# Down projection of a decoder block: seven products for eight on six of eleven weight tiles

## The chip, the cores and the metric

One core of one Trainium2 chip runs the whole block. The core has five engines that run side by side, each through its own queue of instructions in order: TensorE (PE in the profile; PEld is its weight load), VectorE (DVE), ScalarE (ACT), GpSimd (POOL) and SyncE (SP), which here only issues DMAs. The matrix products accumulate in PSUM, eight banks of 128 x 512 fp32 numbers; everything else lies in SBUF. The metric is the device time of one execution in microseconds, the median of several runs.

## What is computed

One layer on 256 tokens of width 1024, all in fp32: two token mixers (a gated linear recurrence and a block-sparse attention) side by side, their merge, a first layer norm, a gated feed-forward network (FFN) and a second layer norm. The part that matters here is the last:

```python
x = layer_norm(DN_ALPHA * x + mixed, ln1_w, ln1_b)
h = jnp.einsum('bsd,df->bsf', x, w_ffn_in)
h_gate, h_up = jnp.split(h, 2, axis=-1)
y = jnp.einsum('bsf,fd->bsd', jax.nn.silu(h_gate) * h_up, w_ffn_down)
return layer_norm(DN_ALPHA * x + y, ln2_w, ln2_b)
```

The hidden width is 2816, that is 22 rows of 128 features. The down projection multiplies 256 x 2816 activations by 2816 x 1024 weights.

## The kernel before

**Halves.** TensorE takes its operands in a rounded 32-bit form (float32r). To keep fp32 accuracy, every operand is split: the high half is a cast on ScalarE, the low half is the operand less that cast, a subtraction on VectorE (`split`, lines 168 to 170). One product of two fp32 matrices is then three matmuls: high by high, high by low, low by high (lines 676 to 678).

**Weights.** `plan` lists all weight tiles in the order of use, 1 MB each (128 partitions x 2048 fp32). `stage` (line 176) loads the next one on SP's queue into one of three `raw` buffers, casts it on ScalarE into one of four `h` buffers (line 192) and subtracts on VectorE into one of four `l` buffers (line 194). `fetch` (line 198) hands out the next staged tile and first stages until three more are ready behind it. So the tile three ahead is written into the buffers of the tile before the current one.

**FFN.** For each pair of feature rows j (line 810) one tile of gate weights and one of up weights are fetched; `wide_pair` makes two PSUM tiles of each (two for the gate from the pool `mm`, two for up from `aux`, four banks each). ScalarE copies half of a PSUM tile out, VectorE adds the other half (lines 817, 818), ScalarE applies the SiLU, VectorE multiplies gate by up, and the product is split into `ah` and `al` for the down projection. The first two pairs are done earlier, for each half of the tokens (`FfnEarly`).

**Down projection.** Eleven tiles q of two feature rows by 1024 columns. For each tile, `rows_pass` multiplies both feature rows, for 128 tokens and for two column halves of 512: eight products of 128 x 128 by 128 x 512 in all, 24 matmuls, into four PSUM banks. For the last three tiles (`HOLD_DOWN`) the products of the second half of the tokens are put off to the end, so that the second layer norm of the first half runs beside them. The last 256 columns of that go to a bank of their own, `more`.

**Second layer norm.** For each half of the tokens: residual times alpha plus PSUM (line 685), statistics (688, 690), a power on GpSimd (692), two scalings with the broadcast weights `wb2` (695, 698), two stores. `bcast` loads such weights through GpSimd's queue.

**Order.** A planner orders the instructions of each engine by a timing model. Inside `tc.manual_schedule(engines=...)` the engines named take their instructions in the order in which the program writes them. Before the change that holds for the output projection and the early FFN pairs, and for TensorE alone in the held part at the end.

**SBUF.** A pool `big` of twelve 8 KB buffers (`slot`) holds the larger arrays; a buffer is handed on when its last reader is done.

Of the kernel before, what the change touches and what calls it, by code (L numbers as in the profile page):

```python
# [71 lines left out]
def plan():  # L72

    tiles = []

    def add(w, k0, kn, c0, n, held=False):
        tiles.append((w, k0, kn, c0 if isinstance(c0, tuple) else (c0,), n, held))

    def feat(w, c0, n):
        for c in range(c0, c0 + n, 256):  # L80
            add(w, 0, 8, c, 256)

    def tok(w, c0, n):
        for c in range(c0, c0 + n, 512):
            add(w, 0, 4, c, 512)
            add(w, 4, 4, c, 512)

    feat("w_in", 0, 1024)
    tok("w_in", 2048, 1024)
    tok("w_in", 3072, 1024)  # L90
    tok("w_in", 6144, 512)
    tok("w_in", 8192, 1024)
    for c in range(2):
        if c == 1:
            tok("w_in", 6144 + 512, 512)
        for j in range(2 * c, 2 * c + 2):
            feat("w_in", 5120 + j * 256, 256)
            feat("w_in", 4096 + j * 256, 256)
    tok("w_in", 7168, 1024)
    tok("w_branch_a", 0, 1024)  # L100
    tok("w_branch_b", 0, 1024)
    for k in range(0, KC, 2):
        add("w_out", k, 2, 0, 1024)
    for j in range(0, EARLY, 2):
        for k in range(0, KC, 4):
            add("w_ffn_in", k, 4, (j * P, FF + j * P), 256, j < HOLD_IN)
    for j in range(EARLY, NF, 2):
        add("w_ffn_in", 0, 8, j * P, 256)
        add("w_ffn_in", 0, 8, FF + j * P, 256)
    for k in range(0, NF, 2):  # L110
        add("w_ffn_down", k, 2, 0, 1024)
    return tiles


# [1 line left out]
def hybrid_layer_kernel(ctx: ExitStack, tc, x, xw, vecs, bias, wts, ln1_w, ln1_b, ln2_w, ln2_b, consts, out):  # L116
# [12 lines left out]
    def slot(name, dt=F32):  # L129
        return big.tile([P, 2048], dt, tag="s8", name=name)  # L130

    def r32(ap):
        return ap.bitcast(F32)
# [27 lines left out]
                return self.pair[self.u, ks, ts]  # L161


    loads = plan()
    ready = []
    state = {"next": 0}

    def split(dst_h, dst_l, src):
        nc.scalar.copy(dst_h, src)
        nc.vector.tensor_sub(dst_l, src, r32(dst_h))  # L170
# [5 lines left out]
    def stage(pieces=None, eng=nc.vector):  # L176
        i = state["next"]
        if i >= len(loads):
            return
        state["next"] += 1  # L180
        _, _, k, _, _, held = loads[i]
        src = wts[i].rearrange("p (k c) -> p k c", k=k)
        view = lambda z: z.rearrange("p (k c) -> p k c", k=k)
        raw = view(wraw.tile([P, 2048], F32, tag="raw", name=f"raw{i}"))
        if held:
            h, l = view(slot(f"wh{i}", F32R)), view(slot(f"wl{i}", F32R))
        else:
            h = view(whi.tile([P, 2048], F32R, tag="h", name=f"wh{i}"))
            l = view(wlo.tile([P, 2048], F32R, tag="l", name=f"wl{i}"))
        for ks in ks_of(pieces or (k,)):  # L190
            nc.sync.dma_start(raw[:, ks, :], src[:, ks, :])
            nc.scalar.copy(h[:, ks, :], raw[:, ks, :])  # L192
            yield
            eng.tensor_sub(l[:, ks, :], raw[:, ks, :], r32(h[:, ks, :]))  # L194
# [465 lines left out]
    def bcast(name, w, b):  # L660
        t = slot(name).rearrange("p (a d) -> p a d", a=2)
        nc.gpsimd.dma_start(t[:, 0, :], w[0].partition_broadcast(P))
        nc.gpsimd.dma_start(t[:, 1, :], b[0].partition_broadcast(P))
        return t
# [12 lines left out]
                    nc.tensor.matmul(ps, lh(kk)[:, ts], wl[:, k, ns], start=False, stop=False)  # L677
                    nc.tensor.matmul(ps, ll(kk)[:, ts], wh[:, k, ns], start=False, stop=(kk == ktot - 1))  # L678

    def layer_norm(name, t, parts, res, wb, r, store=None, more=None):  # L680

        stats = sm.tile([P, len(parts), 6], F32, tag="bst", name=f"{name}s{t}")
        for i, (ps, n0) in enumerate(parts):
            ns = slice(n0, n0 + ps.shape[1])
            nc.vector.scalar_tensor_tensor(r[:, ns], res[:, ns], ALPHA, ps, op0=ALU.mult, op1=ALU.add)
            if more is not None and i == len(parts) - 1:
                nc.vector.tensor_add(r[:, ns], r[:, ns], more)
            nc.vector.bn_stats(stats[:, i, :], r[:, ns])
        ag = sm.tile([P, 4], F32, tag="bag", name=f"{name}a{t}")
        nc.vector.bn_aggr(ag[:, 0:2], stats)  # L690
# [24 lines left out]
    ah = [slot(f"ah{i}", F32R).rearrange("p (k t) -> p k t", k=KC) for i in range(3)]  # L715
    al = [slot(f"al{i}", F32R).rearrange("p (k t) -> p k t", k=KC) for i in range(3)]

    def norm1(t):
        layer_norm("n1", t, pss[t], xr[:, t, :], wb1, x1[:, t, :])
# [11 lines left out]
    class FfnEarly:  # L731
# [74 lines left out]
    e[1][1].transpose()  # L806


    room = slot("room").rearrange("p (i f t) -> p i f t", i=4, f=2)
    for j in range(EARLY, NF, 2):  # L810
        n = j // 2 % 2
        sums = []
        for i, (nm, p, tag) in enumerate([("g", mm, "mm"), ("u", aux, "aux")]):
            pss = wide_pair(f"f{nm}{j}", x1p, p, tag)
            s = room[:, 2 * i + n, :, :]
            for f, ps in enumerate(pss):
                nc.scalar.copy(s[:, f, :], ps[:, 1, :])
                nc.vector.tensor_add(s[:, f, :], ps[:, 0, :], s[:, f, :])
            if i == 0:
                nc.scalar.activation(s, s, AF.Silu)  # L820
            sums.append(s)
        nc.vector.tensor_mul(sums[0], sums[0], sums[1])
        i, k = divmod(j, KC)
        split(ah[i][:, k:k + 2, :], al[i][:, k:k + 2, :], sums[0])

    pss = [row_parts("wd0", [(aux, 512)] * 2), row_parts("wd1", [(aux, 512)] * 2)]
    lhs = (lambda kk: ah[kk // KC][:, kk % KC, :], lambda kk: al[kk // KC][:, kk % KC, :])
    y = slot("y").rearrange("p (t d) -> p t d", t=NT)
    tiles = []
    for q in range(NF // 2):  # L830
        tiles.append((2 * q,) + fetch())
        rows_pass(pss[0], lhs, 0, tiles[-1:], NF)
        if q < NF // 2 - HOLD_DOWN:
            rows_pass(pss[1], lhs, 1, tiles[-1:], NF)
    layer_norm("n2", 0, pss[0], x1[:, 0, :], wb2, y[:, 0, :], store=out[0:P, :])

    left, (bank, n0) = pss[1]
    more = mm.tile([P, 256], F32, tag="mm", name="more")
    held = tiles[-HOLD_DOWN:]
    with tc.manual_schedule(engines={ET.PE}):  # L840
        rows_pass([left, (bank[:, 0:256], n0)], lhs, 1, held, NF)
        rows_pass([(more, n0 + 256)], lhs, 1, held, NF, first=held[0][0])
    layer_norm("n2", 1, [left, (bank[:, 0:256], n0), (bank[:, 256:512], n0 + 256)], x1[:, 1, :], wb2, y[:, 1, :],
               store=out[P:T, :], more=more)


_INS = ['x', 'xw', 'vecs', 'bias', 'wts', 'ln1_w', 'ln1_b', 'ln2_w', 'ln2_b', 'consts']
# [32 lines left out]
```

## Time and profile before

| | |
|---|---|
| median of three runs | 500.73 us (500.57 to 501.01) |
| profiled execution, first to last instruction | 498.3 us |
| TensorE busy | 490.4 us, 2728 matmuls |
| VectorE busy | 355.8 us, 424 instructions |
| ScalarE busy | 265.0 us, 328 instructions |
| HBM read | 91.17 MB |
| FFN's last product, start | 430.8 us |
| down projection's last product, start | 490.93 us |

The profile is one execution, times counted from its first instruction. A timeline row has the start, the duration, the engine, the line, the operation, its output and inputs, and in brackets how long the engine stood idle before it and what released it. Matmuls overlap in the pipe, so the distance from start to start says how fast they go, not the printed duration. In a group's row the numbers behind the bar are busy time in all, mean nanoseconds of one, and idle time before with its releasers. The granted clock is the share of TensorE's full clock that it was allowed.

### The profile page before, as it was taken

The numbers are of one execution on the slowest core, as the hardware profiler recorded it, in microseconds if no ns is written. First come the engines' busy times: TensorE is split into PE (matmuls) and PEld (weight loads), VectorE is DVE, ScalarE is ACT, GpSimd is POOL, SyncE is SP. The second block draws the span as 40 slices with busy tenths as digits, with TensorE's granted clock in tenths as the row PEclk, the third lists the DMA queues.
The fourth block names the chain that finished last, engine by engine and source line by source line (L and its number), as shares of the span: only waits on it lengthen the run. The fifth ranks groups of instructions, "written<-read, shape, count | busy, mean of one in ns | idle before, by whom it ended". The sixth has DMA issues, their size and how long they took to land.

```text
span 498.3 us, 6753 instructions
## 1 busy us (share of the span) xinstructions
PE 490.4 (98%) x2728; PEld 427.8 (86%) x2728; DVE 355.8 (71%) x424; ACT 265.0 (53%) x328; POOL 34.0 (7%) x33
## 2 busy tenths in 40 slices
PE   9999999999999999999999999999999999999994
PEld 9999888888899888888888888888888888888884
DVE  4886799999867796886586778854766656644436
ACT  6794487434547676668654353445655565443300
POOL 0000000000004622331000001000000000000000
PEclk9999999999999999999999999999999999999998
DMA  8967436634442436447664454354654555437002
GB/s 306 422 228 308 169 99 245 232 142 170 168 170 86 170 136 245 151 172 279 244 210 176 166 196 181 110 230 167 236 187 169 191 211 190 168 120 292 13 0 84
DMA packets 14558, 92.65 MB, mean 186 GB/s; under 512 B 1728, under 2 KB 1728, under 8 KB 4672
## 3 DMA queue, kind: packets, MB, share of 16 engines
q1 hardware_dynamic: 13680, 89.08, 48.8%
q0 software_dynamic: 848, 3.15, 1.8%
q8 instruction: 21, 0.34, 0.3%
q14 instruction: 9, 0.07, 0.0%
HBM read 91.17 MB, written 1.05 MB: 185 GB/s over the span
## 4 chain that ended last, share of the span: by engine, by line
PE 98%; DVE 1%; DVEq 0%; issue 0%
PE fu L253 7%; PE fg L253 7%; PE wd L678 4%; PE wd L677 4%; PE wd L676 4%; PE fg L254 3%; PE fu L254 3%; PE mq L253 2%; PE mk L253 2%; PE sc L428 2%; PE hq L265 2%; PE hq L264 2%; PE hq L263 2%; PE za L295 1%; PE za L293 1%; PE mv L293 1%
## 5 line engine op out<-in xcount | busy, mean ns | idle before, releaser
L194 DVE TENSOR_TENSOR wl<-raw,wh 128x2048 fp32r<-128x2048 f32 x77 | 178.1, 2318 | 93.1 <-ACT wh L192 93.0
L192 ACT CAST wh<-raw 128x2048 fp32r<-128x2048 f32 x77 | 146.9, 1917 | 93.8 <-PE wd L678 18.7
L253 PE MATMUL fg<-x1p,wh 128*128 128x512 f32 x144 | 50.5, 394 | 0.0
L253 PE MATMUL fu<-x1p,wh 128*128 128x512 f32 x144 | 50.4, 394 | 0.0
L254 PE MATMUL fg<-x1p,wl 128*128 128x256 f32 x144 | 40.0, 278 | 0.0
L254 PE MATMUL fu<-x1p,wl 128*128 128x256 f32 x144 | 39.9, 277 | 0.0
L678 PE MATMUL wd<-wh,al 128*128 128x512 f32 (+1 forms) x88 | 33.6, 382 | 0.0
L677 PE MATMUL wd<-wl,ah 128*128 128x512 f32 (+1 forms) x88 | 33.6, 382 | 0.0
L676 PE MATMUL wd<-wh,ah 128*128 128x512 f32 (+1 forms) x88 | 33.4, 382 | 0.0
L253 PEld LDWEIGHTS fu<-x1p,wh 128*128 128x128 f32 x144 | 27.0, 187 | 6.2
L253 PEld LDWEIGHTS fg<-x1p,wh 128*128 128x128 f32 x144 | 27.0, 187 | 6.1
L254 PEld LDWEIGHTS fg<-x1p,wl 128*128 128x128 f32 x144 | 27.1, 188 | 0.1
L254 PEld LDWEIGHTS fu<-x1p,wl 128*128 128x128 f32 x144 | 27.1, 188 | 0.0
L676 PEld LDWEIGHTS wd<-wh,ah 128*128 128x128 f32 x88 | 16.5, 188 | 3.3
L677 PEld LDWEIGHTS wd<-wl,ah 128*128 128x128 f32 x88 | 16.5, 188 | 3.2
L678 PEld LDWEIGHTS wd<-wh,al 128*128 128x128 f32 x88 | 16.5, 188 | 3.2
L263 PE MATMUL hq<-xp,wh 128*128 128x256 f32 x64 | 18.1, 283 | 0.0
L264 PE MATMUL hq<-xp,wh 128*128 128x256 f32 x64 | 18.1, 283 | 0.0
L265 PE MATMUL hq<-xp,wl 128*128 128x256 f32 x64 | 18.1, 283 | 0.0
L253 PE MATMUL mk<-xp,wh 128*128 128x512 f32 x48 | 17.5, 402 | 0.0
L253 PE MATMUL mq<-xp,wh 128*128 128x512 f32 x48 | 17.2, 399 | 0.0
L430 DVE COPY_PREDICATED SD<-cst,sc 128x512 f32<-128x512 uint32 x14 | 14.9, 1068 | 1.3 <-PE sc L428 1.0
(269 smaller groups left out, 1192.5 us busy)
## 6 DMA issues: line engine op xcount, KB each, us to landing
raw<-in_wts_dram SPq DMA_DIRECT2D x77, 1024.0 KB, 4.8
xw<-in_xw_dram SPq DMA_DIRECT2D x6, 640.0 KB, 9.3
xr<-in_x_dram POOLq DMA_DIRECT2D x1, 1024.0 KB, 5.5
wb<-in_ln_w_dram POOLq DMA_DIRECT2D x2, 512.0 KB, 5.3
wb<-in_ln_b_dram POOLq DMA_DIRECT2D x2, 512.0 KB, 7.2
out_dram<-y SPq DMA_DIRECT2D x4, 256.0 KB, 2.0
cst<-in_consts_dram SPq DMA_DIRECT2D x1, 960.0 KB, 14.7
xw<-in_xw_dram SPq DMA_DIRECT2D x2, 384.0 KB, 4.0
```

The costliest lines, as they stand in the source:

```text
L192: nc.scalar.copy(h[:, ks, :], raw[:, ks, :])
L194: eng.tensor_sub(l[:, ks, :], raw[:, ks, :], r32(h[:, ks, :]))
L253: nc.tensor.matmul(ps, wh[:, k, wcol], a.both(k), start=(k == 0), stop=False)
L254: nc.tensor.matmul(ps[:, 0, :], wl[:, k, wcol], a[0, k, slice(0, T)], start=False, stop=(k == KC - 1))
L263: nc.tensor.matmul(ps, wh[:, k, wcol], ah[:, kk, :], start=(kk == 0), stop=False)
L264: nc.tensor.matmul(ps, wh[:, k, wcol], al[:, kk, :], start=False, stop=False)
L265: nc.tensor.matmul(ps, wl[:, k, wcol], ah[:, kk, :], start=False, stop=(kk == KC - 1))
L293: nc.tensor.matmul(pss[t], ah[:, kk, ts], wh[:, k, :], start=(kk == 0), stop=False)
L430: nc.vector.copy_predicated(later(SD, n, 4 * g, 4), m[:, None, :, :, :].to_broadcast([P, 4, nb, NT, n]), ps.rearrange("p a (b u i) -> p a ...
L676: nc.tensor.matmul(ps, lh(kk)[:, ts], wh[:, k, ns], start=(kk == first), stop=False)
L677: nc.tensor.matmul(ps, lh(kk)[:, ts], wl[:, k, ns], start=False, stop=False)
L678: nc.tensor.matmul(ps, ll(kk)[:, ts], wh[:, k, ns], start=False, stop=(kk == ktot - 1))
```

## The change

Six tiles of the down projection, q = 2 to 7 (`FAST`), use a scheme of seven products for eight (a Winograd form of Strassen's). A tile's product is read as a 2 x 2 block product: activations in four blocks of 128 x 128 (two halves of the tokens by two feature rows), weights in four corners of 128 x 512 (two feature rows by two column halves).

- **Activations.** In the FFN steps of these tiles VectorE forms four sums and differences of the blocks, each 128 x 128, and the seven blocks are split in halves (896 columns, where 512 were split).
- **Weights.** Each of these tiles is staged twice, from one load. The stage "corners" forms the two differences at once (1024 columns), a further sum and difference (512 each), and splits three corners (1536 columns). The stage "sums" splits the four sums (twice 1024 columns). Both take an `h` and an `l` buffer. The sums lie in constants that are no longer read (`cst`) and in an old buffer (`mv1`).
- **Products.** Three with the corners, four with the sums, three matmuls each. Products 1, 5, 6 and 7 are shared by several outputs and have banks of their own, `p1`, `p5`, `p6`, `p7`; 2, 3 and 4 go straight into the accumulators that plain tiles use too (`p2`, `p3`, `p4`; `wd0` takes plain products alone). All eight banks are in use.
- **Shared products.** After the last of the six tiles `into_residual` adds them into the residual `x1`, which takes its factor alpha there: eight operations of 512 columns on VectorE and a copy on ScalarE. The second layer norm then has alpha 1.
- **Order of tiles.** `DOWN = "SSPSSPSSPPP"`: q = 2, 3, 0, 4, 5, 1, 6, 7, 8, 9, 10. The last three are plain and held as before. The loads follow this order.
- **Written order.** The last two FFN steps and the down projection up to the held part are inside `manual_schedule` for TensorE, VectorE and ScalarE.
- **Moved.** The load of `wb2` goes from before the output projection to behind the FFN; the bank `more` comes from `aux`.

```diff
+ORDERED = 2
+DOWN = "SSPSSPSSPPP"
+FAST = tuple(range(2, 2 + DOWN.count("S")))
...
+    for i, (w, k0, k, _, _, held) in enumerate(plan()):
+        fast = w == "w_ffn_down" and k0 // 2 in FAST
+        loads += [(i, k, held, kind) for kind in (("corners", "sums") if fast else ("plain",))]
...
+    def stage_fast(i, kind):
+        view = lambda z: z.rearrange("p (b c) -> p b c", b=4)
+        h = whi.tile([P, 2048], F32R, tag="h", name=f"wh{kind}{i}")
+        l = wlo.tile([P, 2048], F32R, tag="l", name=f"wl{kind}{i}")
+        if kind == "corners":
+            b = view(wraw.tile([P, 2048], F32, tag="raw", name=f"raw{i}"))
+            nc.sync.dma_start(b, view(wts[i]))
+            y, z = corners[i] = [v.rearrange("p (b c) -> p b c", b=2) for v in (
+                cst[:, C_COS:C_COS + D], cp.tile([P, D], F32, tag="mv1", name=f"sums{i}"))]
+            nc.vector.tensor_sub(y, b[:, 1:3, :], b[:, 0:1, :].to_broadcast([P, 2, 512]))
+            h, l = view(h)[:, 0:3, :], view(l)[:, 0:3, :]
+            nc.scalar.copy(h, b[:, 1:4, :])
+            yield
+            nc.vector.tensor_add(z[:, 0, :], b[:, 2, :], y[:, 0, :])
+            nc.vector.tensor_sub(z[:, 1, :], b[:, 3, :], z[:, 0, :])
+            nc.vector.tensor_sub(l, b[:, 1:4, :], r32(h))
+            yield
+        else:
+            h, l = view(h), view(l)
+            for z, bs in zip(corners.pop(i), (slice(0, 2), slice(2, 4))):
+                nc.scalar.copy(h[:, bs, :], z)
+                yield
+                nc.vector.tensor_sub(l[:, bs, :], z, r32(h[:, bs, :]))
+                yield
+        ready.append((h, l))
...
-    wb2 = bcast("wb2", ln2_w, ln2_b)
...
+        nc.vector.tensor_mul(gate, gate, up)
+        if q in PLAIN:
+            split(act_plain[q][:, 0], act_plain[q][:, 1], gate)
+            return
+        nc.vector.tensor_add(z[:, 4, :], z[:, 0, :], z[:, 2, :])
+        nc.vector.tensor_sub(z[:, 5, :], z[:, 4, :], z[:, 1, :])
+        nc.vector.tensor_sub(z[:, 6, :], z[:, 1, :], z[:, 0, :])
+        nc.vector.tensor_sub(z[:, 7, :], z[:, 3, :], z[:, 5, :])
+        act_fast[q] = fast_parts(FAST.index(q))
+        split(*act_fast[q], z[:, 1:8, :])
...
+    with tc.manual_schedule(engines={ET.PE, ET.DVE, ET.Activation}):
+        for j in range(NF - 2 * ORDERED, NF, 2):
+            ffn_step(j)
+        wb2 = bcast("wb2", ln2_w, ln2_b)
...
+        def fast(q):
+            ah, al = act_fast[q]
+            for products in [((p1, 0, 0), (p2, 2, 2), (p3, 6, 1)),
+                             ((p4, 1, 3), (p5, 3, 0), (p6, 4, 2), (p7, 5, 1))]:
+                wh, wl = fetch()
+                for ps, a, b in products:
+                    stop = q == FAST[-1] and ps in shared
+                    nc.tensor.matmul(ps, ah[:, a, :], wh[:, b, :], start=(q == begins[id(ps)]), stop=False)
+                    nc.tensor.matmul(ps, ah[:, a, :], wl[:, b, :], start=False, stop=False)
+                    nc.tensor.matmul(ps, al[:, a, :], wh[:, b, :], start=False, stop=stop)
+
+        def into_residual():
+            u = slot("u").rearrange("p (b c) -> p b c", b=4)
+            first, second = slice(0, 512), slice(512, D)
+            res = lambda t, ns, z: nc.vector.scalar_tensor_tensor(x1[:, t, ns], x1[:, t, ns], ALPHA, z,
+                                                                  op0=ALU.mult, op1=ALU.add)
+            nc.scalar.copy(u[:, 0, :], p1)
+            res(1, second, p1)
+            nc.vector.tensor_add(u[:, 1, :], p6, u[:, 0, :])
+            nc.vector.tensor_add(u[:, 2, :], p7, u[:, 1, :])
+            nc.vector.tensor_sub(u[:, 3, :], u[:, 1, :], p5)
+            res(1, first, u[:, 3, :])
+            res(0, second, u[:, 2, :])
+            nc.vector.tensor_sub(u[:, 0, :], u[:, 2, :], p5)
+            res(0, first, u[:, 0, :])
...
+        for i, q in enumerate(SEQUENCE):
+            if q in FAST:
+                fast(q)
+                if q == FAST[-1]:
+                    into_residual()
+                continue
+            tile_q = [(2 * q,) + fetch()]
+            if i < len(SEQUENCE) - HOLD_DOWN:
+                for part in late:
+                    rows_pass([part], lhs, 1, tile_q, first=2 * begins[id(part[0])], **ends)
+            else:
+                held += tile_q
+            for part in early:
+                rows_pass([part], lhs, 0, tile_q, first=2 * begins[id(part[0])], **ends)
...
-    more = mm.tile([P, 256], F32, tag="mm", name="more")
+    more = aux.tile([P, 256], F32, tag="aux", name="more")
```

More of the change, by code (lines that the diff above doesn't have):

```diff
@@ L37 @@
 HOLD_DOWN = 3
+ORDERED = 2
+DOWN = "SSPSSPSSPPP"
+FAST = tuple(range(2, 2 + DOWN.count("S")))
+PLAIN = tuple(q for q in range(NF // 2) if q not in FAST)
+SEQUENCE = [(FAST if s == "S" else PLAIN)[DOWN[:i].count(s)] for i, s in enumerate(DOWN)]
 C_ID = 0
@@ L109, in plan @@
         add("w_ffn_in", 0, 8, FF + j * P, 256)
-    for k in range(0, NF, 2):
-        add("w_ffn_down", k, 2, 0, 1024)
+    for q in SEQUENCE:
+        add("w_ffn_down", 2 * q, 2, 0, 1024)
     return tiles
@@ L180, in stage @@
         state["next"] += 1
-        _, _, k, _, _, held = loads[i]
+        i, k, held, kind = loads[i]
+        if kind != "plain":
+            list(stage_fast(i, kind))
+            return
         src = wts[i].rearrange("p (k c) -> p k c", k=k)
@@ L714, in hybrid_layer_kernel, with fast_parts @@
     x1p = Pair("x1p")
-    ah = [slot(f"ah{i}", F32R).rearrange("p (k t) -> p k t", k=KC) for i in range(3)]
-    al = [slot(f"al{i}", F32R).rearrange("p (k t) -> p k t", k=KC) for i in range(3)]
+    apl = [slot(f"ap{i}", F32R).rearrange("p (q u k t) -> p q u k t", q=2, u=2, k=2)
+           for i in range((len(PLAIN) + 1) // 2)]
+    act_plain = {q: apl[i // 2][:, i % 2] for i, q in enumerate(PLAIN)}
+    def fast_parts(i):
+        if i == 0:
+            tiles = [klp.tile([P, H * P], F32R, tag="kl", name="ash"), cp.tile([P, D], F32R, tag="bgr", name="asl")]
+        else:
+            both = slot(f"as{i}", F32R)
+            tiles = [both[:, 0:1024], both[:, 1024:2048]]
+        return [z[:, 0:7 * P].rearrange("p (b t) -> p b t", b=7) for z in tiles]
+    act_fast = {}
     def norm1(t):
@@ L806, in hybrid_layer_kernel, with ffn_step @@
     e[1][1].transpose()
[L809 to L816, printed above, removed]
+    room = slot("room").rearrange("p (n b t) -> p n b t", n=2, b=8)
+    def ffn_step(j):
+        q = j // 2
+        z = room[:, q % 2]
+        gate, up = [z[:, b:b + 4, :].rearrange("p (f t) c -> p f (t c)", f=2) for b in (0, 4)]
+        for nm, p, tag, s in [("g", mm, "mm", gate), ("u", aux, "aux", up)]:
+            for f, ps in enumerate(wide_pair(f"f{nm}{j}", x1p, p, tag)):
@@ L817, in hybrid_layer_kernel @@
                 nc.scalar.copy(s[:, f, :], ps[:, 1, :])
                 nc.vector.tensor_add(s[:, f, :], ps[:, 0, :], s[:, f, :])
-            if i == 0:
+            if nm == "g":
                 nc.scalar.activation(s, s, AF.Silu)
[L821 to L826, printed above, removed]
@@ new lines, in hybrid_layer_kernel @@
+    for j in range(EARLY, NF - 2 * ORDERED, 2):
+        ffn_step(j)
+    with tc.manual_schedule(engines={ET.PE, ET.DVE, ET.Activation}):
+        for j in range(NF - 2 * ORDERED, NF, 2):
+            ffn_step(j)
+        wb2 = bcast("wb2", ln2_w, ln2_b)
+        bank = lambda p, n: p.tile([P, 512], F32, tag="aux" if p is aux else "mm", name=n)
+        p2, p4, p1, p5 = [bank(mm, f"wp{i}") for i in (2, 4, 1, 5)]
+        p7, p3, wd0, p6 = [bank(aux, f"wp{i}") for i in (7, 3, 0, 6)]
+        shared = (p1, p5, p6, p7)
+        lhs = (lambda kk: act_plain[kk // 2][:, 0, kk % 2, :], lambda kk: act_plain[kk // 2][:, 1, kk % 2, :])
+        late, early = [(p2, 512), (p3, 0)], [(p4, 512), (wd0, 0)]
+        ends = dict(ktot=2 * PLAIN[-1] + 2)
+        begins = {id(ps): SEQUENCE[0] for ps in (p2, p3, p4)}
+        begins.update({id(wd0): PLAIN[0]})
+        begins.update({id(ps): FAST[0] for ps in shared})
+        def fast(q):
[22 more added lines that the diff above has]
+            res(0, first, u[:, 0, :])
+        held = []
+        for i, q in enumerate(SEQUENCE):
[8 more added lines that the diff above has]
+                    rows_pass([part], lhs, 1, tile_q, first=2 * begins[id(part[0])], **ends)
+            else:
+                held += tile_q
+            for part in early:
+                rows_pass([part], lhs, 0, tile_q, first=2 * begins[id(part[0])], **ends)
@@ L840, in hybrid_layer_kernel @@
+    y = slot("y").rearrange("p (t d) -> p t d", t=NT)
+    layer_norm("n2", 0, [(wd0, 0), (p4, 512)], x1[:, 0, :], wb2, y[:, 0, :], alpha=1.0, store=out[0:P, :])
+    more = aux.tile([P, 256], F32, tag="aux", name="more")
     with tc.manual_schedule(engines={ET.PE}):
[L841 to L844, printed above, removed]
+        rows_pass([(p3, 0), (p2[:, 0:256], 512)], lhs, 1, held, first=None, **ends)
+        rows_pass([(more, 768)], lhs, 1, held, first=held[0][0], **ends)
@@ L847 @@
+    layer_norm("n2", 1, [(p3, 0), (p2[:, 0:256], 512), (p2[:, 256:512], 768)], x1[:, 1, :], wb2, y[:, 1, :],
+               alpha=1.0, store=out[P:T, :], more=more)
 _INS = ['x', 'xw', 'vecs', 'bias', 'wts', 'ln1_w', 'ln1_b', 'ln2_w', 'ln2_b', 'consts']
```

22 lines of the change are left out of this document (7 added, 15 removed).

## The prediction

> **What bounds the kernel now.** I read the page's first two parts, then the chain that ended last, then the busy times of the last seventy microseconds by stretch, then the timelines of TensorE, VectorE (DVE) and ScalarE (ACT) there.
>
> ```profile
> span 498.3 us, 6753 instructions
> PE 490.4 (98%) x2728; PEld 427.8 (86%) x2728; DVE 355.8 (71%) x424; ACT 265.0 (53%) x328; POOL 34.0 (7%) x33
> PE 98%; DVE 1%; DVEq 0%; issue 0%
> ```
>
> The chain is TensorE from the start nearly to the end. The down projection is the last matrix stage, so its stretches say who has room (columns: length, then busy time of PE, PEld, DVE, ACT, POOL; granted clock; DMA share; GB/s):
>
> ```profile
> 400.00:410.00 10.00, 10.00 (x59) 8.77 (x58) 6.81 (x8) 5.23 (x7) 0.00 (x0) 1.00 0.45 156
> 440.00:450.00 10.00, 10.00 (x45) 8.27 (x45) 5.01 (x3) 5.64 (x3) 0.00 (x0) 1.00 0.29 108
> 460.00:470.00 10.00, 10.00 (x46) 8.29 (x45) 4.59 (x2) 2.95 (x3) 0.00 (x0) 1.00 0.13 54
> 470.00:480.00 10.00, 10.00 (x46) 8.28 (x45) 2.29 (x1) 1.17 (x1) 0.00 (x0) 1.00 0.00 1
> ```
>
> TensorE is full at granted clock 1.00, DVE half idle. The two ends of the stage and its last handover:
>
> ```profile
> 429.91 0.40 PE L253 MATMUL fu<-x1p,wh 128*128 128x512 f32 x1
> ...
> 430.95 0.39 PE L676 MATMUL wd<-wh,ah 128*128 128x512 f32 x1
> ...
> 486.74 0.28 PE L676 MATMUL wd<-wh,ah 128*128 128x256 f32 x1
> ...
> 490.93 0.28 PE L678 MATMUL more<-wh,al 128*128 128x256 f32 x1
> 491.25 0.42 DVE L687 TENSOR_TENSOR y<-y,more 128x256 f32<-128x256 f32 x1 [1.07 <-PE more L678]
> 491.70 0.43 DVE L688 BATCH_NORM_STATS2 n2s<-y 128x6 f32<-128x256 f32 x1
> 492.17 0.24 DVE L690 BATCH_NORM_AGGREGATE n2a<-n2s 128x2 f32<-128x18 f32 x1
> ```
>
> Between 430.95 and 486.74 lie 246 products of 512 columns: 55.79/246 = 0.2268 us each, well under the printed 0.39, which overlaps. The 35 steps from 486.74 to 490.93 make 0.120 us for 256 columns; 429.91 to 430.95 are three pairs of the FFN, 0.347 each. The DVE add of `more` starts 0.2 us after the last product's slot ends (491.05), and from the aggregate at 492.17 to the span's end are 498.3 - 492.17 = 6.13 us, which the change leaves alone. So the end is: that add's start + 0.92 + 6.13.
>
> **The change, part by part.**
>
> *TensorE.* A fast tile issues 3 + 4 products of three matmuls, 21 instead of 24, all of 512 columns. Six tiles save 18 x 0.2268 = **4.08 us**, the ceiling. Weight loads fall in step. The eight accumulators take all eight banks; of the FFN's last banks only those of its last `fu` tile are emptied late (about 432, below), and the products that may need them start after 432.99. I cost that at nothing.
>
> *What DVE and ACT pay.* Durations and queue steps come from these rows of the groups and the timeline:
>
> ```profile
> L194 DVE TENSOR_TENSOR wl<-raw,wh 128x2048 fp32r<-128x2048 f32 x17 | 38.9, 2292 | 39.7 <-ACT wh L192 39.7
> L170 DVE TENSOR_TENSOR fl<-xw,fh 128x1024 fp32r<-128x1024 f32 x6 | 7.4, 1226 | 1.4 <-ACT fh L169 1.3
> L440 DVE TENSOR_TENSOR Tt<-Tt 128x128 f32<-128x128 f32 x1 | 0.3, 291 | 0.0
> L402 DVE TENSOR_TENSOR SD<-sd,cst 128x512 f32<-128x512 f32 x4 | 2.6, 680 | 0.0
> L818 DVE TENSOR_TENSOR room<-fu,room 128x256 f32<-128x256 f32 x11 | 4.6, 417 | 0.0
> L817 ACT COPY room<-fu 128x256 f32<-128x256 f32 x10 | 3.7, 366 | 1.0 <-PE fu L254 1.0
> L169 ACT CAST ah<-room 128x512 fp32r<-128x512 f32 x9 | 5.6, 623 | 3.3 <-DVE room L822 3.2
> L169 ACT CAST fh<-xw 128x1024 fp32r<-128x1024 f32 x6 | 6.3, 1046 | 0.0
> L192 ACT CAST wh<-raw 128x2048 fp32r<-128x2048 f32 x17 | 32.4, 1913 | 33.8 <-PE wd L678 18.7 <-PE fg L253 11.4 <-issue 2.2
> ```
> ```profile
> 443.55 4.49 DVE L194 TENSOR_TENSOR wl<-raw,wh 128x2048 fp32r<-128x2048 f32 x2 [5.84 <-ACT wh L192]
> ...
> 481.50 0.69 DVE L685 SCALAR_TENSOR_TENSOR y<-x,wd 128x512 f32<-128x512 f32 x1 [8.00 <-PE wd L678]
> 482.22 0.69 DVE L688 BATCH_NORM_STATS2 n2s<-y 128x6 f32<-128x512 f32 x1
> 482.86 0.69 DVE L685 SCALAR_TENSOR_TENSOR y<-x,wd 128x512 f32<-128x512 f32 x1
> ...
> 487.27 0.68 DVE L685 SCALAR_TENSOR_TENSOR y<-x,wd 128x512 f32<-128x512 f32 x1
> 487.98 0.69 DVE L688 BATCH_NORM_STATS2 n2s<-y 128x6 f32<-128x512 f32 x1
> ```
>
> Two independent subtractions of 2048 columns take 4.49, so one moves the queue by 4.49 - 2.29 = 2.20, 0.08 under its duration (482.22 to 482.86 shows the same for 512). An operation that needs the one just before it starts 0.03 after that one's end (481.50 + 0.69 to 482.22). No row has 1536 columns: it lies between 1.23 (1024) and 2.29 (2048); as 512 to 1024 adds 0.55 and 1024 to 2048 adds 1.07, twice as much, I take the middle, 1.76. On ACT likewise 1.48. The broadcast operand costs nothing extra in the L402 row.
>
> One fast tile on DVE: differences of corners 1.25 (the next needs it), add 0.71, subtract 0.60, low half of three corners 1.68, two low halves of the sums 2 x 1.14: **6.5 us, where a plain tile has 2.20**. TensorE takes 21 x 0.2268 = 4.76 for that tile and 5.44 for a plain one, so two fast and one plain tile cost DVE 15.2 and TensorE 15.0: **the two engines are level**, and the lead built up before counts. ACT has 1.48 + 2 x 1.05 per fast tile, 9.1 in 15 us, and stays ahead.
>
> *The lead.* Each fetch stages three loads ahead, into the buffers of the load before the current one. In the FFN's last two steps, now in written order, the first corners, sums and second corners are staged, each when a product group of the FFN (16 pairs, 5.55) frees its buffers, and behind the emptying of the group before:
>
> - first corners: group ends 414.3, + 0.2 + copy 0.37 + add 0.45, + 1.25 + 0.71 + 0.60 + 1.76 = 419.6, wanted at 430.95
> - first sums: group ends 419.85, + 0.2 + 0.37 + 0.45 + product 0.71 + cast 0.62 + first sum's cast 0.95 (it steps 0.10 early) + two waits of 0.03 = 423.2, + 1.14 + 1.23 = 425.6, wanted at 433.0
> - second corners: two adds of 0.33 behind that, + 4.32 = 430.6, wanted at 435.7
> - second sums: the same chain as for the first from 430.95 gives 434.3, + 2.37 = 436.7, wanted at 437.75
>
> DVE has no pause of note after that, but for the casts named. Finish against need:
>
> - plain 439.4 (0.5 of it waiting for its cast, which stands behind the sums' two) / 440.5
> - fast 3: corners 443.7 / 445.9, sums 446.0 / 448.0; fast 4: 450.2 / 450.7, 452.5 / 452.7
> - plain 454.7 / 455.4; fast 5: 459.0 / 460.9, 461.2 / 462.9; fast 6: 465.5 / 465.6, 467.8 / 467.7
> - plain 470.0, 472.2, 474.7 against 470.6, 473.3, 476.0
>
> So TensorE stalls about 0.2, at the last sums; its last product ends near 487.4.
>
> *The end.* Moving the shared products into the residual stands on DVE behind the last plain tile's subtraction and before the first normalisation: eight operations of 512 columns, three of them chained, 5.3 us, 474.7 to 479.9. Its input is ready at 470.9. Before, the first normalisation ran from 481.50 to 487.27, 5.77 us, then the second started: 479.9 + 5.77 = 485.7. The second needs 0.71 + 0.64 + 2 x 0.33 + 0.36 = 2.4 to the add: **488.1, against 491.25 before; TensorE alone would allow 487.2 plus the stall of 0.2. DVE ends last by 0.7.** Gain 491.25 - 488.1 = **3.15 us**.
>
> *Edits that I cost at nothing.* Six FFN steps get four 128-column operations (0.29 each by the L440 row) and a split of 896 columns for 512 (about 1.09 for 0.68 on DVE, by even growth): 1.6 us more DVE work per step of 11.1, into the 3.2 of 10 that the row 400 to 410 leaves idle; uncovered, they would cost up to 9.6. The load order changes, its count of eleven does not. The two wide broadcasts of the last normalisation move on POOL's queue from the output projection to the FFN's end; only the tiny power operations stand behind them there.
>
> ```profile
> raw<-in_wts_dram SPq DMA_DIRECT2D x77, 1024.0 KB, 4.8
> ...
> wb<-in_ln_w_dram POOLq DMA_DIRECT2D x2, 512.0 KB, 5.3
> ```
>
> Issued by 432, when a buffer of the FFN's input comes free, they have some 45 us. The `more` bank comes free with the third residual operation, about 477, wanted at 485.
>
> *A rule against the change.* The step of 0.08 under a duration carries a good part of the balance: some 24 independent DVE steps lie on this path. The Trainium skill, page "VectorE: DVE Perf Modes", section "The DRAIN you can't avoid", says that the next operation does not start until the pipe of the one before is empty, unless it is one that nothing holds. By that rule the steps would be whole durations wherever an instruction is held; the trace has a step under the duration (4.49 for two of 2.29) for a subtraction that waits for a cast, so here the measurement decides.
>
> **The rivals.** *DVE pays full durations.* Waits on ACT now stand before many of these operations, and the pairs that show the 0.08 are few. [...] Without it 24 x 0.08 = 1.9 us more: the residual ends at 481.8, the time is 499.4; TensorE then stalls some 1.8 us in front of fast tiles 4 and 6. For it: the balance is that thin. Against: the second of the pair at 443.55 depends on ACT too.
>
> *TensorE keeps the end.* DVE 2% cheaper than summed, or 1536 columns nearer to 1.23: no stall, the add at 487.2: 500.73 - 4.08 = 496.65. This is the lower bound of the forecast. The 1536's upper end, 2.29, on the four fast tiles in the chain would cost 2.1 more, 499.7.
>
> *Slower: the last raw load.* There are three raw buffers; the last plain tile's load waits until the last corners are done (465.5), lands by the row's 4.8 at 470.4, its cast (1.91) ends 472.4, its subtraction stands ahead of all residual work in the queue. Already 0.35 of the 474.7 is this wait. Every further microsecond of landing is a microsecond of the end, and from 3.2 more (8 us) the kernel is slower. A landing like the slowest load of the page,
>
> ```profile
> cst<-in_consts_dram SPq DMA_DIRECT2D x1, 960.0 KB, 14.7
> ```
>
> would give 500.73 + 14.7 - 8.0 = 507.4. Against it: the load before has landed by then, and the DMA engines stand at 0.13 there.
>
> *No change.* The planner, which still orders the other FFN steps, spends what is won: small DVE operations ahead of evacuations, 0.5 us of TensorE's time per fast step: 500.6. Against: TensorE waits nowhere in the FFN now.
>
> **How the numbers follow.** The profiled execution has 498.3; the median of three is 500.73, 2.43 around the span, taken as constant. Forecast 500.73 - 3.15 = **497.6**, own range 496.6 to 498.7 (DVE 2 to 3% either way moves it 0.8 to 1.1): 0.66, with the TensorE-bound end in it. Full durations, 499.4: 0.14, of which 0.10 is faster by over 0.2%. No change: 0.10. Last raw load, slower: 0.10. A measurement of this kernel can tell about 0.2%, 1.0 us. Faster 0.66 + 0.10 = 0.76; same 0.04 + 0.10 = 0.14; slower 0.10. The range takes in the full durations and the 1536's upper end: 496.5 to 499.8, leaving out the slower case and most of no change.
>
> **What would show it.** Right: 228 products of 512 columns after the FFN where 246 were; DVE over 9 of 10 busy from 440 to 480; waits of TensorE on DVE under 0.5 us in all, at the last corners and sums; the second normalisation's first operation near 485.7, and the add of `more` waiting for DVE, not for TensorE. Wrong: a fast tile's DVE work over 7 us; the last plain tile's cast waiting for its load beyond 471; TensorE idle inside the FFN; the first normalisation waiting for its broadcast weights.

## The result and the profile after

The changed kernel takes 497.61 us (median of five runs, 497.45 to 498.18); the kernel before 500.79 in runs on the same chip. The ratio is 0.9938, its 95% interval 0.9926 to 0.995. The forecast was 497.6.

The page of the changed kernel, its span, busy times and chain:

```profile
span 495.9 us, 6795 instructions
PE 486.8 (98%) x2710; PEld 424.4 (86%) x2710; DVE 394.2 (79%) x486; ACT 276.0 (56%) x341; POOL 34.1 (7%) x33
PE 95%; DVE 2%; DMA 1%; issue 0%; ACT 0%; SPq 0%; DVEq 0%
```

TensorE has 18 matmuls fewer (2728 to 2710), DVE 62 operations and 38.4 us more. Where these lie is seen in the stretches of the down projection (length, then busy time of PE, PEld, DVE, ACT, POOL; granted clock; DMA share; GB/s):

```profile
400.00:410.00 10.00, 10.00 (x60) 8.74 (x59) 8.46 (x12) 5.38 (x9) 0.00 (x0) 1.00 0.52 173
440.00:450.00 10.00, 10.00 (x46) 8.29 (x45) 9.86 (x11) 5.15 (x5) 0.00 (x0) 1.00 0.58 211
460.00:470.00 10.00, 10.00 (x46) 8.29 (x45) 9.93 (x9) 6.29 (x5) 0.00 (x0) 1.00 0.52 197
470.00:480.00 10.00, 10.00 (x46) 8.29 (x45) 9.60 (x10) 2.39 (x2) 0.00 (x0) 1.00 0.04 16
```

DVE, half idle here before, is full: 9.93 of 10 where it had 4.59, 9.60 where it had 2.29. TensorE is as full as it was, at clock 1.00, and waits for nothing in this stage. Neither engine has room left there. The two ends of the stage, first on TensorE, then on DVE:

```profile
431.79 0.40 PE L907 MATMUL wp<-whcorners,ash 128*128 128x512 f32 x1
...
487.71 0.28 PE L718 MATMUL more<-wh,ap 128*128 128x256 f32 x1
```
```profile
481.22 0.69 DVE L725 SCALAR_TENSOR_TENSOR y<-x,wp 128x512 f32<-128x512 f32 x1 [0.47 <-PE wp L718]
...
483.92 0.67 DVE L725 SCALAR_TENSOR_TENSOR y<-x,wp 128x512 f32<-128x512 f32 x1
...
488.93 0.41 DVE L727 TENSOR_TENSOR y<-y,more 128x256 f32<-128x256 f32 x1
489.37 0.43 DVE L728 BATCH_NORM_STATS2 n2s<-y 128x6 f32<-128x256 f32 x1
```

From the first product to the add of `more` are 488.93 - 431.79 = 57.14 us; before it was 491.25 - 430.95 = 60.30. I call this **the stage** below. It has become 3.16 us shorter. TensorE's own part, first start to last start, went from 59.98 to 55.92, 4.06 shorter. The add follows the last product's start by 1.22 where it followed by 0.32: DVE ends last, 0.9 behind, and the row of the add has no wait for TensorE any more.

The profiled execution took 498.18, the longest of the five. Its stage starts 0.84 later than before (431.79 against 430.95), so its span shrank by only 2.4 us. The additional DVE work in the FFN is not the cause: 0.82 of the delay is there at the start of the second product group, at 28.69 us where it was 27.87, and from there to the stage are 403.10 us where there were 403.08. A kernel with one more such FFN step (seven fast tiles, below) starts the stage at 430.94. Here the first loads came later, and TensorE waited 0.4 us for casts in its first product group; ScalarE's first cast of `xw` in the two kernels, before and after:

```profile
3.38 0.40 ACT L169 CAST xp<-xw 128x256 fp32r<-128x256 f32 x1 [0.95 <-DMA xw<-in_xw_dram]
```
```profile
3.87 0.41 ACT L178 CAST xp<-xw 128x256 fp32r<-128x256 f32 x1 [1.45 <-DMA xw<-in_xw_dram]
```

In the traces of changed kernels the stage starts anywhere from 430.94 to 431.86; what sets the start was not tried. So I compare stages, not spans, and medians, not single runs.

### The profile page after: what moved, and what is told of

Same layout as the page of the kernel before. It is cut to its first block, busy times and chain, and to the rows that moved or that the text cites. A ratio compares the mean times of both kernels' runs of the same rounds, so it can differ in the third digit from the quotient of the medians.

```text
span 495.9 us, 6795 instructions
## 1 busy us (share of the span) xinstructions
PE 486.8 (98%) x2710; PEld 424.4 (86%) x2710; DVE 394.2 (79%) x486; ACT 276.0 (56%) x341; POOL 34.1 (7%) x33
## 4 chain that ended last, share of the span: by engine, by line
PE 95%; DVE 2%; DMA 1%; issue 0%; ACT 0%; SPq 0%; DVEq 0%
PE fu L293 7%; PE fg L293 7%; PE fg L294 3%; PE fu L294 3%; PE mq L293 2%; PE mk L293 2%; PE sc L468 2%; PE wp L908 2%; PE wp L909 2%; PE wp L907 2%; PE hq L305 2%; PE hq L304 2%; PE hq L303 2%; PE za L334 1%; PE za L333 1%; PE mv L333 1%
## 5 line engine op out<-in xcount | busy, mean ns | idle before, releaser
L206 DVE TENSOR_TENSOR wl<-raw,wh 128x2048 fp32r<-128x2048 f32 x71 | 164.5, 2322 | 57.4 <-ACT wh L204 55.8
L204 ACT CAST wh<-raw 128x2048 fp32r<-128x2048 f32 x71 | 135.5, 1917 | 69.9 <-PE fg L293 11.5
L717 PE MATMUL wp<-wl,ap 128*128 128x512 f32 (+1 forms) x40 | 14.9, 373 | 0.0
L718 PE MATMUL wp<-wh,ap 128*128 128x512 f32 (+1 forms) x40 | 14.9, 373 | 0.0
L716 PE MATMUL wp<-wh,ap 128*128 128x512 f32 (+1 forms) x40 | 14.9, 373 | 0.0
L506 POOL TENSOR_TENSOR ost<-ost,half 128x4 f32<-128x4 f32 x4 | 4.1, 1015 | 154.7 <-DVE ost L505 154.7
L294 PE MATMUL mk<-xp,wl 128*128 128x256 f32 x48 | 13.8, 288 | 0.0
L294 PE MATMUL mq<-xp,wl 128*128 128x256 f32 x48 | 13.6, 284 | 0.0
```

What stands on the lines that cost most here:

```text
L294: nc.tensor.matmul(ps[:, 0, :], wl[:, k, wcol], a[0, k, slice(0, T)], start=False, stop=(k == KC - 1))
L716: nc.tensor.matmul(ps, lh(kk)[:, ts], wh[:, k, ns], start=(kk == first), stop=False)
```

## The experiments

The theory: TensorE's 18 matmuls are worth 4.08 us; DVE is loaded to the brim, gives back 0.9 of it at the end, and its written order is what makes that possible. The rivals: the end is still TensorE's and the lost 0.9 lies elsewhere; DVE has slack; the order is of no weight. The kernel before ran on each batch's chip as well: 500.74, 500.78, 500.83.

| run | median us (runs) | ratio to before [95%] | stage us |
|---|---|---|---|
| the change | 497.61 (5) | 0.9938 [0.9926, 0.995] | 57.14 |
| five fast tiles | 498.43 (4) | 0.9955 [0.9941, 0.997] | 57.82 |
| seven fast tiles | 501.77 (10) | 1.0024 [1.0014, 1.0033] | 61.22 |
| one sum twice | 500.95 (10) | 1.0003 [0.9994, 1.0013] | 60.27 |
| held products in the written block | 497.46 (4) | 0.9937 [0.9922, 0.9952] | 57.02 |
| five, held in the block | 497.67 (5) | 0.9938 [0.9925, 0.995] | 56.92 |
| last load early, held in the block | 497.8 (5) | 0.9943 [0.9929, 0.9956] | 56.99 |
| the same, sums on GpSimd | 507.9 (4) | 1.0142 [1.0128, 1.0155] | 68.24 |
| planner orders DVE and ACT | 499.2 (5) | 0.9968 [0.9956, 0.9981] | 58.46 |
| tail in written order | 496.71 (5) | 0.9918 [0.9904, 0.9931] | 56.23 |
| the change again | 497.63 (5) | 0.9937 [0.9924, 0.9949] | 57.14 |

Against the kernel before, the medians and the stages (one trace each) give the same difference within 0.35 us, except with the sums on GpSimd, where they are 0.8 apart.

**Five fast tiles.** One fast tile becomes plain: TensorE 3 matmuls more, DVE 4.3 us less.

```diff
-DOWN = "SSPSSPSSPPP"
+DOWN = "SSPSSPSPPPP"
```

> Five fast tiles, in the order SSPSSPSPPPP. Theory (VectorE and TensorE are level at six tiles, VectorE's queue ends last by 0.7 to 1 us): TensorE saves only 15 x 0.2268 = 3.40 us, but VectorE now has pauses, the add of `more` starts 0.2 us behind TensorE's last product: 500.8 - 3.4 = 497.4, no slower than six tiles. Rival (TensorE's count of products sets the time, VectorE is off the path): 0.68 us slower than six, 498.3.

Measured: 498.43, the rival's number, for a reason that neither named. DVE had room, but could not use it:

```profile
473.94 2.28 DVE L206 TENSOR_TENSOR wl<-raw,wh 128x2048 fp32r<-128x2048 f32 x1
481.80 0.69 DVE L725 SCALAR_TENSOR_TENSOR y<-x,wp 128x512 f32<-128x512 f32 x1 [5.58 <-PE wp L718]
...
489.51 0.40 DVE L727 TENSOR_TENSOR y<-y,more 128x256 f32<-128x256 f32 x1
```

DVE stands idle 5.58 us before the first normalisation, waiting for products of the last tile's first token half. The held products are a block of their own, and the planner drew 13 of them ahead of these. So freeing DVE of 4.3 us bought nothing, and the end lies 1.22 behind the last product (488.29) as with six.

**Seven fast tiles.** One plain tile becomes fast: TensorE's count falls by 3 more (0.68 us), DVE has 6.5 - 2.2 = 4.3 more.

```diff
-DOWN = "SSPSSPSSPPP"
+DOWN = "SSPSSSSSPPP"
```

> Seven fast tiles, in the order SSPSSSSSPPP. Theory: 4.3 us more of VectorE's work where it is already full; TensorE stands still some 5 us in front of fast tiles, and the time is 501.9, slower than before the change. Rival (TensorE's count sets the time): 0.68 us faster than six, 496.9.

Measured: 501.77, stage 61.22, 4.08 longer than with six. TensorE now waits (the waits on TensorE from 430 on: total, times, longest):

```profile
PE wp L908 <- DVE wlcorners L227: 3.4, 3, 1.2
```

From its first start to its last TensorE takes 60.00 us, where 55.92 less 0.68 would do without waits: 4.8 lost, about the 5 that the theory named. The matmuls saved are still saved, but of the 4.3 us that the tile adds to the full DVE 4.08 come back at the end. The theory holds.

**One sum twice.** A measured dose: the subtraction that makes the third sum is written a second time in all six fast tiles, 6 x 0.72 = 4.3 us of DVE work.

```diff
             nc.vector.tensor_sub(z[:, 1, :], b[:, 3, :], z[:, 0, :])
+            nc.vector.tensor_sub(z[:, 1, :], b[:, 3, :], z[:, 0, :])
```

> The second weight difference of each fast tile is written twice, 6 x 0.7 us more on VectorE, the result unchanged. Theory (no room on VectorE once its lead is used): about 2.4 us of the 4.3 reach the end, 500.0, and TensorE waits some 2.5 us in front of fast tiles. Rival (VectorE is off the path): 497.6 as with the change.

Measured: 500.95, 3.3 more than the change; stage 60.27, 3.13 more. The whole gain is gone, and the rival that DVE has slack falls. The theory gave 2.4: it let too much of the dose vanish. How much arrives is seen at the plain tile in the middle, in the change and with the dose:

```profile
453.21 2.28 DVE L206 TENSOR_TENSOR wl<-raw,wh 128x2048 fp32r<-128x2048 f32 x1
```
```profile
454.64 2.28 DVE L206 TENSOR_TENSOR wl<-raw,wh 128x2048 fp32r<-128x2048 f32 x1
```

Counted from each stage's own start (431.79 and 431.27) it comes 21.42 and 23.37 us in: 1.95 later after four doses. Two doses fall ahead of the stage and all but 0.5 of them is lost there (the plain tile before stands at 6.16 and 6.66); the two in the stage count in full, 2 x 0.72. Two more make 1.95 + 1.44 = 3.39, and the last three subtractions do begin 3.40 later. At the end 3.13 are left: the 0.47 that the first normalisation waited for TensorE in the change is gone, and the residual's chain pauses 0.46 where it paused 0.11. DVE has slack in the FFN, and none behind it.

**Held products in the written block.** Their block and `more` move into the large one, so nothing is drawn ahead.

```diff
+        more = aux.tile([P, 256], F32, tag="aux", name="more")
+        rows_pass([(p3, 0), (p2[:, 0:256], 512)], lhs, 1, held, first=None, **ends)
+        rows_pass([(more, 768)], lhs, 1, held, first=held[0][0], **ends)
     y = slot("y").rearrange("p (t d) -> p t d", t=NT)
...
-    more = aux.tile([P, 256], F32, tag="aux", name="more")
-    with tc.manual_schedule(engines={ET.PE}):
-        rows_pass([(p3, 0), (p2[:, 0:256], 512)], lhs, 1, held, first=None, **ends)
-        rows_pass([(more, 768)], lhs, 1, held, first=held[0][0], **ends)
```

> The held products stand in the same written order as the tiles before them, so the planner cannot pull thirteen of them ahead of the last tile's first-half products. Theory (VectorE's chain ends last, its first normalisation waited 0.5 us for those products): it starts 0.4 to 0.5 us earlier, 497.2, if TensorE does not wait for the last tile. Rival (the pulled products filled waits of TensorE for VectorE): TensorE waits 0.2 to 0.5 us in front of the last tiles, 497.6 or more.

Measured: 497.46, not to be told from the change; stage 57.02. The first normalisation no longer waits for TensorE (479.74 instead of 481.22), but another wait took the place:

```profile
482.24 0.69 DVE L728 BATCH_NORM_STATS2 n2s<-y 128x6 f32<-128x512 f32 x1
483.69 0.69 DVE L725 SCALAR_TENSOR_TENSOR y<-x,wp 128x512 f32<-128x512 f32 x1 [0.75 <-PE wp L718]
484.29 0.20 DVE L730 BATCH_NORM_AGGREGATE n2a<-n2s 128x2 f32<-128x12 f32 x1
```

The planner, which still orders the tail on DVE, puts the second normalisation's first operation ahead of the first one's aggregate, and its held products are now late.

**Five fast tiles with held in the block.** Both edits together: DVE has room and can use it.

> Five fast tiles, and the held products in written order behind the tiles. Theory (with five tiles the late end came from the held products that the planner pulled ahead: the first normalisation could only start 6.5 us before TensorE's last product and its chain to the add of `more` takes 7.7): it now starts 8.4 us before TensorE's end, the add follows TensorE's last product by 0.2, 497.5. Rival (VectorE's tail is too long whatever the order): 498.3 as without the order.

Measured: 497.67, as the theory had it. Now the add waits for TensorE:

```profile
488.78 0.42 DVE L727 TENSOR_TENSOR y<-y,more 128x256 f32<-128x256 f32 x1 [1.07 <-PE more L718]
```

The stage is 56.92, 3.38 shorter than before: 15 x 0.2268 = 3.40. **When DVE keeps up, what remains is the count of matmuls.** It also shows that five and six tiles are worth the same as long as the sixth's 0.68 is lost at the end.

**The last load early.** The last plain tile's raw data gets a buffer of its own, so its load no longer waits for the last corners (beside held in the block).

```diff
-        raw = view(wraw.tile([P, 2048], F32, tag="raw", name=f"raw{i}"))
+        last = i == wts.shape[0] - 1
+        raw = view(slot(f"raw{i}") if last else wraw.tile([P, 2048], F32, tag="raw", name=f"raw{i}"))
```

> Six fast tiles, held products in written order, and the last plain tile's raw load in a buffer of its own, so that it need not wait for the last corners. Theory (that wait leaves VectorE idle only 0.2 to 0.3 us): 497.2, against 497.5 without. Rival (this load is what ends last): its cast moves from 471.1 to behind the casts before it, 469.3, and up to 1.0 us is gained, 496.5.

Measured: 497.8, stage 56.99 against 57.02. The three last subtractions close up, 6.69 us for the three where they took 6.92, but the wait in the tail grows by about the same:

```profile
483.23 0.69 DVE L726 SCALAR_TENSOR_TENSOR y<-x,wp 128x512 f32<-128x512 f32 x1 [0.94 <-PE wp L719]
```

0.75 became 0.94: what DVE won there, it waited away in the tail. Neither the theory's 497.2 nor the rival's 496.5 came: the last load costs nothing by itself in this form.

**Sums on GpSimd.** The same kernel with the two 512-column sums of every fast tile on GpSimd, 1.3 us off DVE per tile.

```diff
-            nc.vector.tensor_add(z[:, 0, :], b[:, 2, :], y[:, 0, :])
-            nc.vector.tensor_sub(z[:, 1, :], b[:, 3, :], z[:, 0, :])
+            nc.gpsimd.tensor_add(z[:, 0, :], b[:, 2, :], y[:, 0, :])
+            nc.gpsimd.tensor_sub(z[:, 1, :], b[:, 3, :], z[:, 0, :])
```

> As the run before, and the two 512-column sums of each fast tile on GpSimd, which is idle there (1.3 us each by its rows of that size). Theory: 1.3 us less on VectorE per fast tile gives it pauses, TensorE's last product is the end: the add of `more` 0.2 us behind it, 500.74 - 4.08 = 496.7. Rival (GpSimd's longer chain delays the casts of the sums, or slows VectorE): TensorE waits in front of the sums, 497.5 or more.

Measured: 507.9, 11 us worse than expected; the theory was wrong here. One fast tile on GpSimd, then on DVE:

```profile
440.81 2.69 POOL L226 TENSOR_TENSOR sums<-raw,cst 128x512 f32<-128x512 f32 x1 [7.84 <-issue]
443.57 2.14 POOL L227 TENSOR_TENSOR sums<-raw,sums 128x512 f32<-128x512 f32 x1
```
```profile
440.58 1.75 DVE L228 TENSOR_TENSOR wlcorners<-raw,whcorners 128x1536 fp32r<-128x1536 f32 x1
442.25 2.32 DVE L235 TENSOR_TENSOR wlsums<-cst,whsums 128x1024 fp32r<-128x1024 f32 x1
446.84 1.23 DVE L235 TENSOR_TENSOR wlsums<-sums,whsums 128x1024 fp32r<-128x1024 f32 x1 [2.26 <-ACT whsums L233]
```

The two engines take turns. GpSimd's first sum begins while DVE splits the corners (to 442.33) and ends 1.17 after that, at 443.50; DVE's next operation, 1.22 long, ends 1.07 after this, at 444.57; GpSimd's second ends 1.14 after that, at 445.71. Then the cast of that sum can begin, and DVE has been idle 2.26. One tile takes DVE 8.53 us (439.45 to 447.98) where it took 6.52, though 1.3 us of work is gone from it. The Trainium skill's page "SBUF — State Buffer", section "Who interferes with whom", says that a DVE instruction with two SBUF inputs contends with a GpSimd instruction that reads SBUF, because its second input comes through a read interface that they share, and that the sharing is an exclusive lock. The trace agrees: each end above follows the last one by about one operation's own length. The port is not the whole of the loss, though. The sums stand in a chain from GpSimd over ScalarE to DVE, and one takes GpSimd 1.30 us even undisturbed where DVE takes 0.69; what that chain would cost without the sharing was not tried. Some 2.5 us more come from a lower granted clock (last section).

**The planner orders DVE and ScalarE.** The large block stays in written order for TensorE alone.

```diff
-    with tc.manual_schedule(engines={ET.PE, ET.DVE, ET.Activation}):
+    with tc.manual_schedule(engines={ET.PE}):
         for j in range(NF - 2 * ORDERED, NF, 2):
```

> The last two feed-forward steps and the down projection in written order for TensorE alone; the planner orders VectorE and ScalarE. Theory (the amount of VectorE's work, not its order, sets the end): the same work in another order, 497.6 to 498.5. Rival (the written order brings the gain): TensorE waits for tiles that are staged too late, 499.5 or more.

Measured: 499.2, between theory and rival; stage 58.46, 1.32 longer. DVE does the same operations in another order, and one half of the sums comes late:

```profile
453.65 0.39 PE L907 MATMUL wp<-whsums,as 128*128 128x512 f32 x1
455.70 0.50 PE L908 MATMUL wp<-wlsums,as 128*128 128x512 f32 x1 [1.66 <-DVE wlsums L234]
```

The step is 2.05 instead of 0.23. The written order of these two engines is worth 1.3 to 1.6 us, about half of the gain.

**The tail in written order.** Held in the block, the last load early, and both token halves of the second layer norm on DVE in one order written out: residual to its end, the first normalisation through its aggregate and first factor, the second one's first operation, the first one's last factor, then the rest of the second.

```diff
+        def norm_steps(t, parts, store, more=None):
+            r, res = y[:, t, :], x1[:, t, :]
...
+            for ns, (ps, _) in zip(cut, parts):
+                nc.vector.scalar_tensor_tensor(r[:, ns], res[:, ns], 1.0, ps, op0=ALU.mult, op1=ALU.add)
+                yield
...
+        one = norm_steps(0, [(p4, 512), (wd0, 0)], out[0:P, :])
+        two = norm_steps(1, [(p3, 0), (p2[:, 0:256], 512), (p2[:, 256:512], 768)], out[P:T, :], more)
+        for s in [one] * 5 + [two] + [one] + [two] * 7:
+            next(s)
```

> As the run with the raw load and the held products (six fast tiles), and VectorE's operations of both second normalisations in one written order: the first one's first, without the second one's first operation standing in it, which waited there 0.9 us for TensorE. Theory (VectorE's tail ends last by 0.7 to 1.0 us behind TensorE): the add of `more` follows TensorE's last product by 0.2 to 0.3, 56.2 to 56.4 us behind the stage's first product instead of 57.0, and the time is 496.9. Rival (the tail's length does not depend on that order): 497.6.

Measured: **496.71**, the best of all (496.57 to 497.03; the change again on the same chip, 497.42 to 498.11, so the two sets of five do not touch). TensorE's last product and DVE's add:

```profile
487.37 0.28 PE L719 MATMUL more<-wh,ap 128*128 128x256 f32 x1
```
```profile
486.70 1.01 DVE L957 BATCH_NORM_STATS2 n2s<-y 128x6 f32<-128x512 f32 x2
487.68 0.42 DVE L956 TENSOR_TENSOR y<-y,more 128x256 f32<-128x256 f32 x1
```

The add follows the last product's start by 0.31, as in the kernel before (0.32), and DVE has just become free: both engines arrive together. The stage, 56.23, is 4.07 shorter than before, and the time 4.12: TensorE's ceiling of 4.08 is reached. From the run with the last load early (497.8, stage 56.99) it differs by the written tail alone; the written tail without the early load was not tried.

**The change again**, unaltered, for that comparison.

> The changed kernel once more, for comparison on the same chip: 497.6; the add of `more` 57.1 us behind the stage's first product.

Measured: 497.63, stage 57.14, both as in the first runs.

## Why the prediction was right, point by point

**TensorE.** 4.08 us were forecast, 4.06 came. The five-tile run with held in the block, with 3.38 for 15 matmuls, confirms the price of one.

**DVE per fast tile.** 6.5 us forecast. The timeline of one such tile after the change:

```profile
446.69 1.22 DVE L221 TENSOR_TENSOR cst<-raw 128x1024 f32<-128x1024 f32 x1
447.94 0.69 DVE L225 TENSOR_TENSOR sums<-raw,cst 128x512 f32<-128x512 f32 x1
448.67 0.69 DVE L226 TENSOR_TENSOR sums<-raw,sums 128x512 f32<-128x512 f32 x1
449.27 1.75 DVE L227 TENSOR_TENSOR wlcorners<-raw,whcorners 128x1536 fp32r<-128x1536 f32 x1
450.94 1.22 DVE L234 TENSOR_TENSOR wlsums<-cst,whsums 128x1024 fp32r<-128x1024 f32 x1
452.08 1.22 DVE L234 TENSOR_TENSOR wlsums<-sums,whsums 128x1024 fp32r<-128x1024 f32 x1
453.21 2.28 DVE L206 TENSOR_TENSOR wl<-raw,wh 128x2048 fp32r<-128x2048 f32 x1
```

446.69 to 453.21 are 6.52. The 1536 columns, whose size no row had shown, take 1.75 (1.76 taken, in the middle between two rows). The steps of the independent operations are 0.08 to 0.09 under their durations, though each subtraction of a low half needs a cast of ScalarE: 450.94 to 452.08 is 1.14 for 1.22. (The pair of 512 columns that the prediction set beside it, 482.22 to 482.86, has 0.05.) So the rival of full durations falls. The Trainium skill's page "VectorE: DVE Perf Modes", section "The DRAIN you can't avoid", does not stand against these steps: it says that a next operation that is not held starts earlier. The page judges "held" by where an operation's inputs and output start among the partitions, and a wait does not count. The prediction took a wait for a cast to be such a hold, which was a misreading. The operations here all begin at the first partition, so by the page none is held, and the trace's 1.14 for 1.22 agrees.

**The table of finish against need.** The rows of after stand 0.84 later than before by their start. With that taken off, the plain subtractions end at 439.4, 454.65, 469.9 and 474.7 (forecast 439.4, 454.7, 470.0, 474.7), and the residual at 480.75 - 0.84 = 479.9 (forecast 479.9).

**The stall of 0.2 at the last sums** did not come, because two times in its comparison were a little off. The last sums were forecast done at 467.8 and wanted at 467.7. They were done at 467.33 + 1.22 - 0.84 = 467.7, and the low half, which DVE makes, is wanted only by the second matmul of the first product. In the change the planner put a held product of a plain tile (L716) between the two:

```profile
468.56 0.39 PE L907 MATMUL wp<-whsums,as 128*128 128x512 f32 x1
468.78 0.39 PE L716 MATMUL wp<-wh,ap 128*128 128x512 f32 x1
469.01 0.39 PE L908 MATMUL wp<-wlsums,as 128*128 128x512 f32 x1
```

That was not needed. With the held products in the written block nothing stands between, and the step is 0.23 all the same:

```profile
468.47 0.40 PE L907 MATMUL wp<-whsums,as 128*128 128x512 f32 x1
468.70 0.40 PE L908 MATMUL wp<-wlsums,as 128*128 128x512 f32 x1
```

The same drawing ahead, 13 of the 18 products of one bank, cost later.

**The end: the sum was right because two errors cancelled.** The prediction started the first normalisation with the residual's end, let it run 5.77 us, and put 2.4 of the second behind it: 8.15 in all, from 479.9 to 488.1. In fact the first operation waited 0.47 for TensorE, which the prediction had put at nothing, since held products had been drawn ahead of the ones it needs, and the two normalisations lie interleaved on DVE (the second's first operation at 483.92, or 483.1 by the old start, not 485.7), 7.71 in all. 479.9 + 0.47 + 7.71 = 488.1. That the two errors were of one size was luck. The mechanism, DVE ending last, was right; the shape of the tail was not. In the prediction both blocks kept their order; outside the large block the planner had a say on both engines, and I had not asked what it would draw ahead. The tail run shows what this is worth: 0.9 us.

**Where DVE ends** was forecast 0.7 behind TensorE and came 0.9 behind, because the stall did not come and TensorE ended 0.2 earlier.

**The last raw load.** The last plain tile's cast waited for it, and DVE for the cast, 0.26 (0.35 forecast):

```profile
471.27 1.91 ACT L204 CAST wh<-raw 128x2048 fp32r<-128x2048 f32 x1 [1.94 <-DMA raw<-in_wts_dram]
```

The cast's start, 471.27 - 0.84 = 470.4, is the landing as forecast, so the slower case stayed away.

**No change by the planner in the FFN.** DVE has 8.46 of 10 in the stretch 400 to 410, 1.65 more than before, and TensorE stays full: from the second product group to the stage it takes 0.02 us longer than before. Where the planner was given the last two steps and the down projection too, it did cost 1.3 to 1.6, but by late sums in the down projection, not in the FFN, where the rival put the loss.

## What to carry to other kernels

Fewer matmuls paid for with work on another engine count in full only while that engine has room: sum its work tile by tile against TensorE's time, with the lead at the start, and where the two are level expect nearly every further microsecond to come back. Then look at the end, where the order of the last operations decides who arrives last: putting both engines' tails into one written order gave 0.9 us here, which neither a lighter load on DVE nor an earlier transfer gave by itself. A total that comes out right does not show that the order was understood: here the tail's wait and its length were both wrong by half a microsecond, in opposite directions. And an engine that stands idle is no free room where it must share a port with the one that is full.

## What the hardware showed unexpectedly

**GpSimd and DVE excluded each other** for whole operations in the run with the sums on GpSimd, where both read two operands from SBUF: a 1024-column DVE subtraction took 2.32 us instead of 1.22, a 512-column GpSimd sum 2.69 instead of 1.30, which is what the one that began while DVE stood idle took:

```profile
427.83 1.30 POOL L226 TENSOR_TENSOR sums<-raw,cst 128x512 f32<-128x512 f32 x1 [6.68 <-ACT room L870]
```

This was the only run whose theory missed by more than 2 us.

**The granted clock fell after one pause and not after its twin.** In the run with sums on GpSimd TensorE paused twice in the same way: 2.46 and 1.03 us beyond the usual step from 452.67 on, and 2.50 and 1.03 from 472.53 on. The stretches behind the first and the second pause:

```profile
454.00:456.00 2.00, 0.49 (x1) 0.19 (x1) 0.66 (x1) 1.74 (x2) 0.23 (x1) 1.00 0.38 57
456.00:458.00 2.00, 1.38 (x6) 1.16 (x7) 1.42 (x2) 2.00 (x2) 0.00 (x0) 1.00 0.90 377
```
```profile
474.00:476.00 2.00, 0.67 (x1) 0.19 (x1) 0.76 (x1) 1.83 (x2) 0.14 (x1) 0.86 0.00 0
476.00:478.00 2.00, 1.48 (x4) 1.20 (x5) 1.42 (x2) 2.00 (x2) 0.00 (x0) 0.50 0.00 0
478.00:480.00 2.00, 2.00 (x6) 1.63 (x5) 2.00 (x2) 2.00 (x2) 0.00 (x0) 0.50 0.00 0
```

The granted clock (first number behind the busy times) stayed 1.00 the first time. The second time it fell at about 475.4, when the longer pause was just over and the shorter still to come (its mean is 0.93 from 475.0 to 475.5 and 0.50 from there to 476), and was back at about 482.2. In these 7 us a matmul stepped 0.427 instead of 0.227, some 2.5 us lost. Why the one and not the other was not tried; shorter pauses, up to 1.8 us beyond the step in the run where the planner orders DVE and ScalarE, left it at 1.00.
